# Attention stage: both transposed halves of a unit in one burst, and four more planner steps at the start

## The chip, the core and the metric

The kernel runs on one core of a Trainium2 chip. The core has a matrix engine (TensorE, PE in the profile, with its weight loads as PEld), a vector engine (DVE), a scalar engine (ACT), GpSimd (POOL), and a sync engine (SP) that issues most transfers. Each engine takes its instructions in order; they wait for each other by semaphores. Matrix products go into PSUM, from which ACT and DVE read them.

The metric is the time of one execution in device microseconds; the median of several runs counts. A profile is of one further execution, whose own time stands beside its span below.

## What is computed

One transformer-like block on a sequence of 1024 tokens, width 1024: a modulated RMS norm, one wide projection, attention beside a bidirectional state-space scan, a gated merge, and an MLP. The part that matters here is the attention: 16 query heads over 4 key heads, head width 64, all in float32, and the sigmoid gates that are merged later.

```python
q, k, v, xBC, z, dt_raw, gates = jnp.split(proj, offsets, axis=-1)
...
def one_block(qi):
    sc = jnp.einsum("bqgrd,bkgd->bgrqk", qi, k).astype(jnp.float32) * scale
    p = jax.nn.softmax(sc, axis=-1).astype(v.dtype)
    return jnp.einsum("bgrqk,bkgd->bqgrd", p, v)
...
g_attn = jax.nn.sigmoid(gates[..., :D_MODEL])
g_ssd = jax.nn.sigmoid(gates[..., D_MODEL:])
merged = g_attn * (attn @ w_attn_out[l]) + g_ssd * (ssd @ w_ssd_out[l])
```

## The kernel before

The kernel goes through stages: projections, convolution, attention, scan with the attention's output product, merge, and the MLP. To keep float32 accuracy with faster products, a matrix is often split into a high part (rounded by ACT, `A.copy` at L173) and the rest (a subtraction on DVE, `tt` at L159); the helper `split` does both, so these two lines stand for many places, and the tiles' names tell them apart.

The change is in the attention stage. Two generators, each a stream of PE work, are interleaved there:

- `attn_stream` goes through 128 **units**: 16 heads by 8 blocks of 128 queries. Four units make a **band** of 512 queries.
- `gates_stream` computes columns of the gate projection, 11 blocks of 16 steps, three matmuls a step (tile `psg`, L211 to L213; in the text G). Its weights are loaded by SP (L186), split by ACT and POOL; its results are copied by ACT (`ost`, L1006) and stored from ACT's queue.

`weave` (the planner) sees only the costs that the streams yield. Each stream has a total; at each point the one whose share of its total is smaller goes on until its next yield. The stage is a manual schedule for PE: PE's instructions stand in its queue in exactly the order in which the streams issue them. The instructions of the other engines are ordered when the program is built, by when their inputs and buffers are ready, those written earlier first.

For a unit u the stream does:

- `scores(u)`, S in the text: four matmuls of 512 columns into a PSUM tile `pss` (L1042, L1044; two such tiles); DVE takes the negative row maximum `nm` (L1046); ACT writes the exponentials into `pf` (L1048; two such tiles) and their sums. S runs two units ahead.
- `turn(u, hf)`, T0 and T1: for each half of the 1024 keys four 128 x 128 transposes of `pf` into a PSUM tile `pst` (L1059). There are two `pst`; one comes free when `split` has made `ph` (ACT) and `pl` (DVE) of it. A buffer of a tag goes to whichever tile asks next once one is free. `ph` and `pl` hold one half of a band (four units side by side), with three buffers each, so a band takes two.
- `values(b, hf)`, V: the second products, 16 matmuls a band, given out four at a time by `all_values`. They come one band after the transposes, in the four units of the next band, and are summed in the one tile `pv` (L1096 to L1099). The first four matmuls and the next four (units 4k and 4k+1 of the next band) read the first half's `ph` and `pl`, the others the second half's. After the last, ACT copies `ax` and DVE adds `av`. The first four units have no V, since no band is complete.
- once a head, at every eighth unit, `sums`: one transpose of the reciprocal sums into a `pst` tile (L1070; Z in the text), copied by ACT as `zr`; then loads and POOL's division.

In the order before, V and any G that the planner gives out stand between T0 and T1. Totals: 128 x 2.72 + 18 for the attention (a unit yields 0.92 for S, 0.44 for each half, 0.92 for V), 114.4 for the gates (176 steps at 0.65).

Of the kernel before, what the change touches and what calls it, by code (L numbers as in the profile page):

```python
# [34 lines left out]
GATES_EARLY = 11  # L35
LEAD2 = 0
# [4 lines left out]
L0 = 18  # L41
# [22 lines left out]
def weave(tc, *streams, lead=0):  # L64


    st = [[g, float(total), 0.0, i] for i, (g, total) in enumerate(streams)]
    while st:
        for s in sorted(st, key=lambda e: e[2] / e[1]):
            try:  # L70
                if s[3] == 0 and lead:
                    with tc.high_priority(offset=lead):
                        cost = next(s[0])
                else:
                    cost = next(s[0])
            except StopIteration:
                st.remove(s)
                break
            if cost is not None:
                s[2] += cost  # L80
                break
        else:
            raise RuntimeError("no stream can go on")
# [8 lines left out]
def block(ctx: ExitStack, tc: tile.TileContext, ia, out, upto=99, dbg=None):  # L92
    nc = tc.nc
    V, A, G, T = nc.vector, nc.scalar, nc.gpsimd, nc.tensor
# [77 lines left out]
    def split(hi, lo, src, e_hi=None, e_lo=None):  # L172
        (e_hi or A.copy)(hi, src)  # L173
        tt(e_lo or V, lo, src, hi.bitcast(F32), ALU.subtract)
# [17 lines left out]
    def w_cols(w, c0, k0=0):  # L192
        return w[k0 * P:(k0 + KT) * P, c0:c0 + P].rearrange("(k p) c -> p k c", p=P)

    def gemm_cm(ps_pool, tag, wsrcs, ahi, alo, evac, bufs=None, pair=False, then=None, e_lo=None):

        ws = {0: load_w(wsrcs[0], e_lo=e_lo)}
        if then:
            then()
        n = len(wsrcs)  # L200
        order = [(i, h) for i in range(n) for h in range(2)]
        if pair:
            order[:4] = [(0, 0), (1, 0), (0, 1), (1, 1)]
        for i, half in order:
            if half == 0 and i + 1 < n and i + 1 not in ws:
                ws[i + 1] = load_w(wsrcs[i + 1], e_lo=e_lo)
            hi, lo = ws[i]
            if 1:
                ps = ps_pool.tile([P, 512], F32, name=tag, tag=tag, bufs=bufs)
                for k in range(KT):  # L210
                    T.matmul(ps, hi[:, k], ahi[k][half], start=k == 0, stop=False)  # L211
                    T.matmul(ps, hi[:, k], alo[k][half], start=False, stop=False)  # L212
                    T.matmul(ps, lo[:, k], ahi[k][half], start=False, stop=k == KT - 1)  # L213
                    yield 0.65
                evac(i, half, ps)
# [783 lines left out]
    with tc.tile_pool(name="p3k", bufs=1, reuse_waits="tile") as p3k, \  # L999
# [3 lines left out]
        def gates_stream(pool, psp, i0, i1, bufs=2, e_lo=None):  # L1003
            def evac(i, half, ps):
                st = pool.tile([P, 512], F32, name="ost", tag="ost", bufs=2)
                A.copy(st, ps)  # L1006
                adma(gt_d[i0 + i][:, half * 512:(half + 1) * 512], st)

            yield from gemm_cm(psp, "psg", [w_cols(w_in, OFF_G + i * P) for i in range(i0, i1)], hhi, hlo, evac, bufs=bufs, e_lo=e_lo)

        def attn_stream():
# [5 lines left out]
            def load_head(h):  # L1017
                g = h // 4
                if h % 4 == 0:
                    k1, k2, v1 = (p3k.tile(shp, F32R, name=nm, tag=nm, bufs=2)  # L1020
                                  for nm, shp in (("k1", [P, S]), ("k2", [P, S]), ("v1", [P, NT, P])))
                    dma(k1.bitcast(F32), k1_d[g])
                    kv[g] = k1, k2, v1
                qs[h] = p3k.tile([P, S], F32R, name="q1", tag="q1", bufs=2)
                dma(qs[h].bitcast(F32), q1_d[h])
                if h % 4 == 0:
                    dma(k2.bitcast(F32), k2_d[g])
                    dma(v1.bitcast(F32), v1_d[g])
# [6 lines left out]
            def scores(u):  # L1035
                h, t = divmod(u, NT)
                q1 = qs[h]
                k1, k2, _ = kv[h // 4]
                ps = ps3.tile([P, S], F32, name="pss", tag="pss", bufs=2)
                ts = slice(t * P, (t + 1) * P)  # L1040
                for n in range(2):
                    T.matmul(ps[:, n * 512:(n + 1) * 512], q1[:, ts], k1[:, n * 512:(n + 1) * 512], start=True, stop=False)  # L1042
                for n in range(2):
                    T.matmul(ps[:, n * 512:(n + 1) * 512], q1[:, ts], k2[:, n * 512:(n + 1) * 512], start=False, stop=True)  # L1044
                nm = nms.pop() if nms else p3.tile([P, 1], F32, name="nm", tag="nm", bufs=4)
                V.tensor_reduce(out=nm, in_=ps, axis=AX.X, op=ALU.max, negate=True)  # L1046
                pfs[u] = p3.tile([P, S], F32, name="pf", tag="pf", bufs=2)
                A.activation(pfs[u], ps, AF.Exp, bias=nm, accum_out=zall[:, u:u + 1])  # L1048

            def turn(u, hf):  # L1050

                pf = pfs[u]
                b, j = divmod(u, 4)
                if j == 0:
                    phs[b, hf] = p3.tile([P, 4, 512], F32R, name="ph", tag="ph", bufs=3)
                    pls[b, hf] = p3.tile([P, 4, 512], F32R, name="pl", tag="pl", bufs=3)
                pt = ps3.tile([P, 4, P], F32, name="pst", tag="pst", bufs=2)
                for k in range(4):
                    T.transpose(pt[:, k], pf[:, (hf * 4 + k) * P:(hf * 4 + k + 1) * P], ident)  # L1059
                js = slice(j * P, (j + 1) * P)  # L1060
                split(phs[b, hf][:, :, js], pls[b, hf][:, :, js], pt)
# [3 lines left out]
            def sums(h):  # L1065

                zi = p3.tile([P, NT], F32, name="zi", tag="zi", bufs=1)
                V.reciprocal(zi, zall[:, NT * h:NT * h + NT])
                pz = ps3.tile([P, 4, P], F32, name="pst", tag="pst", bufs=2)
                T.transpose(pz[0:NT, 0], zi, ident)  # L1070
                zr = p3.tile([NT, P], F32, name="zr", tag="zr", bufs=1)
                A.copy(zr, pz[0:NT, 0])
                adma(rz_d[h].rearrange("(t p) -> t p", p=P), zr)

            def sums_back(h):

                rzs[h] = p3.tile([HD, S], F32, name="rz", tag="rz", bufs=1)
                dma(rzs[h], rz_d[h].partition_broadcast(HD))

            def divide(b):  # L1080
                h, av, hs = b // 2, avs.pop(b), slice((b % 2) * 512, (b % 2 + 1) * 512)
                tt(G, av, av, rzs[h][:, hs], ALU.mult)

                (adma if h == NH - 1 else dma)(av_d[h // 2][(h % 2) * HD:(h % 2 + 1) * HD, hs], av)
# [25 lines left out]
            def all_values(b):  # L1110
                for hf in range(2):
                    yield from values(b, hf)

            NU = NH * NT
# [7 lines left out]
            pvq = iter(())  # L1122
            for u in range(NU + 4):
                if u % NT == 4 and 1 < u // NT + 1 < NH:
                    load_head(u // NT + 1)
                if u + 2 < NU:
                    scores(u + 2)
                    yield 0.92
                for hf in range(2):
                    if u < NU:  # L1130
                        turn(u, hf)
                        yield 0.44
                    if hf == 0:
                        c = next(pvq, None)
                        if c:
                            yield c
                h = u // NT - 1
                if h >= 0:
                    if u % NT == 0:
                        sums(h)  # L1140
                    elif u % NT == 1:
                        sums_back(h)
                    elif u % NT in (2, 3):
                        divide(2 * h + u % NT - 2)
                if u % 4 == 3 and u < NU:
                    pvq = all_values(u // 4)

        with tc.manual_schedule(engines=M2):
            weave(tc, (attn_stream(), 128 * 2.72 + L0), (gates_stream(p3, ps3, 0, GATES_EARLY, 1, G), GATES_EARLY * 10.4), lead=LEAD2)
    if upto <= 3:  # L1150
        return dict(gt_d=gt_d, av_d=av_d, rz_d=rz_d)

# [896 lines left out]
```

## Time and profile before

| what | us |
|---|---|
| median of 3 runs | 2447.72 (2446.38 to 2450.83) |
| the profiled execution, its own time | 2451.32 |
| span of the profile | 2449.5 |
| PE busy in the span | 2377.3 |
| DVE busy | 1702.4 |
| ACT busy | 1091.8 |
| POOL busy | 827.9 |
| the attention stage, from the first transpose to the last | 685.3 to 1176.2 |

The span is that of the instructions in the trace; the 1.8 us to the execution's own time lie around it. Busy times of PE overlap from one matmul to the next, so that a full PE shows as 97% or more and small waits inside it do not show at once. In a timeline row stand the start, the length, the engine, the line, the operation, what is written from what, the shape and the count; in brackets the idle time of the engine before it and what ended it.

### The profile page before, as it was taken

To read this page: it belongs to the slowest core of one execution; us is meant where nothing else is said; L and a number is where in the kernel's file an instruction comes from. 1 tells how busy PE (TensorE), PEld (TensorE's weight loads), DVE (VectorE), ACT (ScalarE), POOL (GpSimd) and SP (SyncE) were. 2 spreads that over 40 slices of the span, in tenths; PEclk is the share of its full clock that TensorE was granted. 3 is DMA by queue.
4 is the path that set the end of the run, shared out by engine and by line. 5 is a ranking of instruction groups with operands and counts; after the bars stand their busy time and mean duration, and the time that the engine had idled before them with its cause. 6 is when DMAs were issued, how large, how long until landed. Compare 5 with 4: busy or idle time off the path is not lost.

```text
span 2449.5 us, 32244 instructions
## 1 busy us (share of the span) xinstructions
PE 2377.3 (97%) x11307; PEld 1899.4 (78%) x11307; DVE 1702.4 (69%) x2325; ACT 1091.8 (45%) x1884; POOL 827.9 (34%) x637
## 2 busy tenths in 40 slices
PE   8999999999989999999989999999999999999999
PEld 4998877888867777777767767787787888788887
DVE  5876435777756666666577796557568888768794
ACT  5455413555566666666333343344242222364430
POOL 0221107666611111110356666534006786123200
PEclk9999999999999999999999999999999999999999
DMA  7664841333531212111667765476325554654422
GB/s 255 181 184 147 259 167 65 95 104 112 185 112 52 91 52 81 57 54 48 219 205 228 221 208 176 146 270 205 132 74 194 185 197 163 234 171 138 157 79 82
DMA packets 288595, 366.53 MB, mean 150 GB/s; under 512 B 33961, under 2 KB 168849, under 8 KB 288433
## 3 DMA queue, kind: packets, MB, share of 16 engines
q1 hardware_dynamic: 216246, 288.77, 37.2%
q10 hardware_dynamic: 72187, 75.70, 9.3%
q8 instruction: 90, 1.47, 0.2%
q14 instruction: 72, 0.59, 0.1%
HBM read 250.54 MB, written 113.84 MB: 149 GB/s over the span
## 4 chain that ended last, share of the span: by engine, by line
PE 80%; DVE 8%; DMA 5%; issue 2%; ACT 2%; POOL 2%; SPq 0%; ACTq 0%; DVEq 0%; POOLq 0%
PE pst L1059 5%; PE psg L211 4%; PE psg L213 4%; PE psg L212 4%; PE p L1928 3%; PE p L1927 3%; PE p L1926 3%; PE psc L919 3%; PE psc L920 3%; PE psc L921 3%; PE psq L519 3%; PE psq L520 3%; PE psq L518 3%; PE pp L1514 3%; PE pp L1512 3%; PE pp L1513 3%
## 5 line engine op out<-in xcount | busy, mean ns | idle before, releaser
L1046 DVE TENSOR_REDUCE nm<-pss 128x1 f32<-128x1024 f32 x128 | 156.7, 1225 | 125.1 <-PE pss L1044 123.5
L1048 ACT ACTIVATE pf<-pss,nm 128x1024 f32<-128x1024 f32 x128 | 143.0, 1117 | 98.8 <-PE pst L1059 96.1
L159 DVE TENSOR_TENSOR pl<-pst,ph 128x512 fp32r<-128x512 f32 x256 | 167.6, 683 | 27.1 <-ACT ph L173 27.1
L1059 PEld LDWEIGHTS pst<-masks,pf 128*128 128x128 f32 x1024 | 117.8, 140 | 73.8 <-issue 33.9
L519 PE MATMUL psq<-twl,hh 128*128 128x512 f32 (+1 forms) x448 | 168.3, 377 | 2.5 <-DVE twl L159 2.5
L1059 PE MATMUL pst<-masks,pf 128*128 128x128 f32 x1024 | 157.4, 276 | 13.3 <-DVE pl L159 10.8
L173 ACT CAST ph<-pst 128x512 fp32r<-128x512 f32 x256 | 145.9, 586 | 54.5 <-PE pst L1059 37.9
L518 PE MATMUL psq<-twh,hh 128*128 128x512 f32 (+1 forms) x448 | 166.8, 376 | 3.5 <-ACT twh L173 3.5
L520 PE MATMUL psq<-twh,hl 128*128 128x512 f32 (+1 forms) x448 | 167.4, 375 | 0.0
L159 POOL TENSOR_TENSOR av<-av,rz 64x512 f32<-64x512 f32 x32 | 42.0, 1315 | 346.4 <-DMA rz<-rz 141.2
L1926 PE MATMUL p<-o,o 128*128 128x512 f32 x400 | 153.6, 390 | 3.3 <-ACT o L173 1.9
L1927 PE MATMUL p<-o,o 128*128 128x512 f32 x400 | 155.3, 389 | 0.2 <-DVE o L159 0.2
L1928 PE MATMUL p<-o,o 128*128 128x512 f32 x400 | 153.7, 389 | 0.0
L173 ACT CAST wop<-ws 128x512 fp32r<-128x512 f32 x116 | 71.2, 621 | 127.5 <-PE pp L1514 52.4
L865 DVE SCALAR_TENSOR_TENSOR tap<-pad,cwT,tap 128x1024 f32<-128x1024 f32 x96 | 123.4, 1285 | 4.9 <-ACT tap L863 3.5
L159 POOL TENSOR_TENSOR ws<-r,r 128x512 f32<-128x512 f32 x29 | 41.7, 1438 | 215.2 <-DVE ro L159 151.0
L159 POOL TENSOR_TENSOR sl<-sl 128x512 f32<-128x512 f32 x32 | 49.6, 1553 | 179.1 <-DVE o L159 72.7
L173 ACT CAST o<-sl 128x512 fp32r<-128x512 f32 x92 | 56.9, 622 | 104.7 <-PE p L1928 88.7
L1097 PE MATMUL pv<-pl,v 128*64 128x512 f32 x256 | 101.5, 417 | 0.0
L159 DVE TENSOR_TENSOR o<-sl,o 128x512 fp32r<-128x512 f32 x92 | 72.3, 788 | 39.8 <-ACT o L173 39.8
L211 PE MATMUL psg<-hh,whi 128*128 128x512 f32 x224 | 95.3, 425 | 1.2 <-ACT ost L1006 1.2
L518 PEld LDWEIGHTS psq<-twh,hh 128*128 128x128 f32 x448 | 84.8, 189 | 14.6 <-ACT twh L173 3.9
(457 smaller groups left out, 7026.4 us busy)
## 6 DMA issues: line engine op xcount, KB each, us to landing
ar<-r SPq DMA_DIRECT2D x100, 256.0 KB
wada<-in_w_ada_dram SPq DMA_DIRECT2D x48, 512.0 KB
r<-in_w_mlp_dram SPq DMA_DIRECT2D x32, 512.0 KB
sl<-in_w_mlp_dram SPq DMA_DIRECT2D x64, 256.0 KB
r<-in_w_in_dram SPq DMA_DIRECT2D x26, 512.0 KB
r<-ro ACTq DMA_DIRECT2D x49, 256.0 KB
r<-as SPq DMA_DIRECT2D x48, 256.0 KB
xb<-cst ACTq DMA_DIRECT2D x20, 512.0 KB
```

What stands on the lines that cost most here:

```text
L159: e.tensor_tensor(out=o, in0=a, in1=b, op=op)
L173: (e_hi or A.copy)(hi, src)
L211: T.matmul(ps, hi[:, k], ahi[k][half], start=k == 0, stop=False)
L518: T.matmul(o, hhi[k][half][:, sl], hi[:, k % 2, :n], start=k == 0, stop=False)
L519: T.matmul(o, hhi[k][half][:, sl], lo[:, k % 2, :n], start=False, stop=False)
L520: T.matmul(o, hlo[k][half][:, sl], hi[:, k % 2, :n], start=False, stop=k == KT - 1)
L1046: V.tensor_reduce(out=nm, in_=ps, axis=AX.X, op=ALU.max, negate=True)
L1048: A.activation(pfs[u], ps, AF.Exp, bias=nm, accum_out=zall[:, u:u + 1])
L1059: T.transpose(pt[:, k], pf[:, (hf * 4 + k) * P:(hf * 4 + k + 1) * P], ident)
L1926: T.matmul(ps, a[:, 0, sl], b[0], start=start, stop=False)
L1927: T.matmul(ps, a[:, 0, sl], b[1], start=False, stop=False)
L1928: T.matmul(ps, a[:, 1, sl], b[0], start=False, stop=stop)
```

## The change

Both halves of a unit are transposed one behind the other, with one yield of 0.88 for the two; V comes after them. In units 0 to 3, where there is no V, the stream yields 0.92 all the same without issuing anything, so that the planner gives out gate products there. The attention's total grows by these four yields.

```diff
                 if u + 2 < NU:
                     scores(u + 2)
                     yield 0.92
-                for hf in range(2):
-                    if u < NU:
-                        turn(u, hf)
-                        yield 0.44
-                    if hf == 0:
-                        c = next(pvq, None)
-                        if c:
-                            yield c
+                if u < NU:
+                    turn(u, 0)
+                    turn(u, 1)
+                    yield 0.88
+                c = next(pvq, 0.92 if u < 4 else None)
+                if c:
+                    yield c
...
-            weave(tc, (attn_stream(), 128 * 2.72 + L0), (gates_stream(p3, ps3, 0, GATES_EARLY, 1, G), GATES_EARLY * 10.4), lead=LEAD2)
+            weave(tc, (attn_stream(), 128 * 2.72 + 4 * 0.92 + L0), (gates_stream(p3, ps3, 0, GATES_EARLY, 1, G), GATES_EARLY * 10.4), lead=LEAD2)
```

## The prediction

> **What bounds the kernel now.** I read the shares of the chain that ended last, then the table by stretches of time over the attention stage, then the timeline of single units and the list of waits. In the table the columns are the stretch, its length, the busy time of PE, its weight loads, DVE, ACT and POOL, the granted clock, and the DMA share with its GB/s.
>
> ```profile
> PE 80%; DVE 8%; DMA 5%; issue 2%; ACT 2%; POOL 2%; SPq 0%; ACTq 0%; DVEq 0%; POOLq 0%
> ```
>
> ```profile
> 685.00:698.00 13.00, 8.99 (x53) 7.02 (x53) 8.86 (x11) 7.98 (x15) 0.00 (x0) 1.00 0.16 48
> 698.00:1177.00 479.00, 468.86 (x2482) 355.21 (x2481) 327.14 (x419) 319.05 (x571) 60.92 (x39) 1.00 0.20 60
> 1182.00:1245.00 63.00, 53.01 (x211) 39.02 (x209) 42.48 (x56) 18.11 (x32) 26.28 (x24) 0.92 0.86 280
> ```
>
> In the steady part (698 to 1177 us) PE is the only full engine; DVE and ACT are busy for about two thirds of it, DMA for a fifth. So a change of the order counts only by PE's waits. "Busy" hides some of them, because a matmul lasts longer than the step to the next. I therefore count by steps. The chain of waits gives 0.23 us for a matmul of 512 columns (two in 0.47) and 0.109 us for a transpose (16 in 1.75):
>
> ```profile
> 857.12 0.47 PE pss L1042 x2
> ```
>
> ```profile
> 1771.84 1.75 PE pst L1543 x16
> ```
>
> A **band** is four units, whose second products (V, four matmuls a unit) come one band later. Per unit the order is scores S (four matmuls), transposes T0 and T1 (four each, the halves), V, and gate products G (three matmuls) wherever the planner's fractions put them. By the yields that is 2.72/366.16 x 114.4/0.65 = 1.31 G a unit, 5.23 a band. The timeline of one unit 4k+1, the second of a band (start, length, engine, line):
>
> ```profile
> 858.08 1.23 DVE L1046 TENSOR_REDUCE nm<-pss 128x1 f32<-128x1024 f32 x1 [1.14 <-PE pss L1044]
> ...
> 858.57 0.60 PE L1059 MATMUL pst<-masks,pf 128*128 128x128 f32 x4
> ...
> 858.92 0.48 PE L1097 MATMUL pv<-pl,v 128*64 128x512 f32 x1
> ...
> 859.21 0.59 ACT L173 CAST ph<-pst 128x512 fp32r<-128x512 f32 x1 [0.79 <-PE pst L1059]
> 859.24 0.40 PE L1099 MATMUL pv<-ph,v 128*128 128x512 f32 x1
> ...
> 859.71 0.39 PE L1099 MATMUL pv<-ph,v 128*128 128x512 f32 x1
> 859.82 0.69 DVE L159 TENSOR_TENSOR pl<-pst,ph 128x512 fp32r<-128x512 f32 x1 [0.52 <-ACT ph L173]
> 860.19 0.59 ACT L173 CAST ph<-pst 128x512 fp32r<-128x512 f32 x1 [0.40 <-PE pv L1099]
> 860.57 0.66 PE L1059 MATMUL pst<-masks,pf 128*128 128x128 f32 x4 [0.47 <-DVE pl L159]
> 860.81 0.69 DVE L159 TENSOR_TENSOR pl<-pst,ph 128x512 fp32r<-128x512 f32 x1 [0.29 <-ACT ph L173]
> ```
>
> Four transposes cost 0.44 here: from 858.57 to the second matmul behind them at 859.24 is 0.67, less one matmul step. The same place (T0 of a unit 4k+1) in the second band and thirty bands later:
>
> ```profile
> 703.29 0.60 PE L1059 MATMUL pst<-masks,pf 128*128 128x128 f32 x4
> ...
> 703.49 1.22 DVE L1046 TENSOR_REDUCE nm<-pss 128x1 f32<-128x1024 f32 x1 [1.69 <-PE pss L1044]
> ...
> 704.63 0.68 DVE L159 TENSOR_TENSOR pl<-pst,ph 128x512 fp32r<-128x512 f32 x1
> ...
> 705.36 0.66 PE L1059 MATMUL pst<-masks,pf 128*128 128x128 f32 x4
> ```
>
> ```profile
> 1167.92 0.60 PE L1059 MATMUL pst<-masks,pf 128*128 128x128 f32 x4
> ```
>
> A band takes (1167.92 - 703.29)/30 = 15.49 us. Its work is 32 matmuls of S and V plus 15.7 of G at 0.23 (10.97), and eight bursts at 0.44 (3.52): 14.5. So PE waits **0.98 us a band**, 30 us over 31 bands. This is all that any order of this stage can win.
>
> **The change part by part.** First, the burst by itself. Eight transposes at 0.109 and two bursts of four at 0.44 are both 0.88 us; joining them saves nothing. No instruction is added or removed, and no DMA: the gate weights' loads and the gates' stores shift with their products by under a unit.
>
> Second, what no longer lies between the halves.:
>
> ```profile
> ACT ph L173 <- PE pv L1099: 15.9, 31, 1.1
> PEld pst L1059 <- DVE pl L159: 15.6, 34, 1.0
> PE pst L1059 <- DVE pl L159: 10.8, 18, 1.6
> ```
>
> PE and its weight loads wait for DVE's pl, and ACT's copy ph waits for a V matmul 31 times, once a band. The reason is in the code: ph and pl have three buffers, a band takes two, and the second of the new band gets the one that V of units 4k and 4k+1 still reads. So ph of unit 4k's second half can be written only after V(4k+1). Until then its PSUM tile, one of the two named pst, stays taken (860.19: ph starts after V's last matmul). T1(4k+1) therefore gets the pst buffer of T0(4k+1): it starts at 860.57, right after that half's pl (859.82 to 860.51), and before the older one (860.81). From T0's last start (858.90, three steps of 0.11 after 858.57) the way is: fill 0.27 (the 0.60 of the row less 0.33), ph 0.59, pl 0.69, and three hand-overs: 1.67 us. At 703.29 no G stood between S and T0, the row maximum was on DVE when ph was done, and the way is 1.74 (703.62 to 705.36).
>
> Before, V(4k+1) and often a G ran in that time. After, T1 stands directly behind T0, and V(4k+1) behind T1 on PE's queue. T1 cannot have the other buffer at all, since that waits for V(4k+1). So **PE stands for 1.67 to 1.74 less one step of 0.11** in each of 31 bands. Writing out the order that the yields give, 17 of them have S directly before T0 (1.63) and 14 a G between (1.56): mean 1.60.
>
> Behind the waiting T1 on PE stand V(4k+1), a G, and S(4k+4); ph(4k,1) waits for that V, pl for ph, and the next burst T(4k+2) for pl. How ACT orders such work, one half earlier, is seen here: the exponential first, then both ph, then both pl, then a burst:
>
> ```profile
> 853.60 1.12 ACT L1048 ACTIVATE pf<-pss,nm 128x1024 f32<-128x1024 f32 x1 [0.55 <-PE pst L1059]
> ...
> 854.70 1.06 ACT L173 CAST ph<-pst 128x512 fp32r<-128x512 f32 x2
> ...
> 855.67 1.28 DVE L159 TENSOR_TENSOR pl<-pst,ph 128x512 fp32r<-128x512 f32 x2
> ...
> 856.49 0.63 PE L1059 MATMUL pst<-masks,pf 128*128 128x128 f32 x4
> ```
>
> From T1's last start (0): exponential 0.32 to 1.42; V directly behind T1 ends at 1.19; ph(4k,1) 1.42 to 2.00; pl 2.04 to 2.72. PE meanwhile does V, G, S and reaches T(4k+2) at 2.64: it waits 0.14, and its second half 0.17 for the second pl. With the G before the V, V ends at 1.88 and pl at 3.22; PE arrives at 2.64 (wait 0.64 + 0.17), or with a second G at 3.33 (0.12). Counted in the order: 18 x 0.31, 3 x 0.81, 9 x 0.12, so 0.29 a band.
>
> The other two bursts of a band lose a wait. Now T1's pst has to come back through exponential, ph and pl by the next T1, which costs about 0.1 in many units (856.49 is such a one: the G matmul before it started at 856.15). After, ph of the first half can go before the exponential, and 2.6 us of V, G and S lie between bursts. I take 0.40 a band for all that is left there: the eighth unit's Z transpose, which now meets a pst buffer still in use (0.3 to 1), V's buffer pv waiting for av, and the gate copies. Bounds: nothing, and the 0.98 that a whole band waits today.
>
> Third, the first four units, which have no V. Before, their halves stand together or with one G between:
>
> ```profile
> 691.35 0.60 PE L1059 MATMUL pst<-masks,pf 128*128 128x128 f32 x4
> ...
> 693.52 0.63 PE L1059 MATMUL pst<-masks,pf 128*128 128x128 f32 x4 [1.57 <-DVE pl L159]
> ```
>
> This row also shows on the chip what two halves in one burst do when no pst is free: 1.57 us idle. The new costs bring five G into these units in place of three. Followed through with the same durations, the scores of unit 4 come 0.3 us later with 2 x 0.69 = 1.4 us more done: a gain of 1 us, with bounds 0 and 1.4. At the tail, the last two bursts have no S before them and pl(124,1) comes late: a loss of about 2 (bounds 0 and 3).
>
> **Sum.** A band: 14.5 + 1.60 + 0.29 + 0.40 = 16.8 against 15.49, +1.31; times 31 is +41; -1 at the start, +2 at the tail: **+42 us**. The stage behind begins with loads that are issued as the attention's buffers come free, and nothing in it absorbs a later start. The profiled execution took 2451.32 (span 2449.5), so 2493 by it; the median of the runs is 3.6 lower, so **2490 us**.
>
> **Rivals.** (a) Faster. If T1(4k+1) found a free pst, through ph(4k,1) no longer waiting for V or PE passing V before T1, the burst would cost nothing, most waits of 0.1 would go, and with 0.29 to 0.40 left of 0.98 a band the stage would win 20 us: 2427. Against it: the 31 waits, and the place in the order. It decides where T1 starts less than 1.1 us after T0's last start; the rows say 1.67. Chance 0.04.
>
> (b) No change: the 31 new waits (50 us) are balanced by the 30 us of today's and 20 more that I fail to see: 2448. Against it, PE has no more idle time in the stage. Chance 0.02.
>
> (c) Slower by less: all other waits vanish, 31 x (1.56 - 0.98) = +18: 2466. Chance 0.12. (d) Slower by more: T(4k+2) always pays 0.81 and the rest 0.98: 31 x (1.63 + 0.81 + 0.98 - 0.98) = +76, 2523. Chance 0.12.
>
> (e) The clock falls. In 1182 to 1245, with waits and a DMA share of 0.86, it was 0.92; at that rate the 450 us of PE work (31 x 14.5) would take 39 more: 2529. Against it, 685 to 698 holds two waits of about 1.6 and was granted 1.00. Chance 0.02. The Trainium skill, "TensorE: Matmul & The Clock Gate", HAM oscillation, puts the fall of the clock at PE gaps over about 3.4 us; the 1.00 row agrees, and by that rule (e) would have no chance. The same page, A second HAM failure mode: psum-queue depth-cycling, says that short but frequent idling between matmul groups can make the clock swing too, which speaks against this change; no row before shows it.
>
> **How the numbers follow.** My forecast has 0.68. The range goes from (c) to (d), 2466 to 2523. A measurement of this kernel tells 0.2%, 5 us, from no change; chances: faster 0.04, within 0.02, slower 0.94.
>
> **What would show it.** In the changed profile T1 of each unit 4k+1 starts 1.67 to 1.75 after T0's last start with nothing between, released by DVE's pl, and a band takes about 16.8 us. ACT's ph still waits for PE's pv 31 times, now longer. Wrong would be a PE order in which V stands between the halves, a T1 released at once, or a band under 15.5.

## The result and the profile after

The changed kernel takes 2527.44 us (median of 4 runs, 2526.75 to 2528.62) against 2447.32 of the kernel before (median of 4, 2446.38 to 2450.83): a ratio of 1.0325, with an interval of 1.0313 to 1.0338, or 80 us more. The forecast was 2490 with a range up to 2523. The sign and the first wait came out as forecast. The forecast size, 42 us, was about half of the measured one, because a second wait was put far too small.

The page of the changed kernel, its busy times (share of the span, instructions):

```profile
PE 2381.2 (94%) x11307; PEld 1907.1 (76%) x11307; DVE 1708.5 (68%) x2325; ACT 1092.2 (43%) x1884; POOL 828.4 (33%) x637
```

The work is the same (PE 2381.2 against 2377.3 us), but PE's share of the span falls from 97% (2377.3 of 2449.5) to 94%. The profiled execution took 2526.75, its span is 2524.8: 75.3 us longer than before.

The table by stretches of the changed kernel (stretch, length, busy time of PE, weight loads, DVE, ACT and POOL, granted clock, DMA share, GB/s):

```profile
685.00:698.00 13.00, 13.00 (x78) 11.04 (x77) 10.85 (x14) 10.92 (x22) 0.92 (x1) 1.00 0.13 35
...
698.00:1255.00 557.00, 472.99 (x2468) 363.39 (x2467) 324.83 (x417) 317.24 (x567) 59.09 (x39) 1.00 0.17 52
```

The start (685 to 698) is now full: 13.00 of 13.00 where PE was busy for 8.99. The steady part, which now reaches to about 1255, has PE busy for 473 of 557 us at a granted clock of 1.00. So the lost time is PE standing still, and it isn't the clock. The list of waits of the changed kernel over the stage (who waits for whom: us, times, the longest):

```profile
ACT ph L173 <- PE pst L1059: 138.6, 117, 2.6
...
PE pst L1059 <- DVE pl L159: 78.1, 63, 2.2
...
PEld pst L1059 <- DVE pl L159: 72.3, 61, 2.5
...
ACT ph L173 <- PE pv L1099: 4.3, 11, 0.4
```

PE's transposes wait for DVE's pl 63 times for 78.1 us; before it was 18 times for 10.8. That is about twice a band, where the forecast had one long wait a band. The timeline shows both (first the start of the stage, then unit 37, a 4k+1, and unit 38, a 4k+2; the rows at 699.35 and 1239.47 are T0 of units 5 and 125):

```profile
690.28 1.03 PE L1059 MATMUL pst<-masks,pf 128*128 128x128 f32 x8
...
699.35 0.60 PE L1059 MATMUL pst<-masks,pf 128*128 128x128 f32 x4
...
844.25 0.60 PE L1059 MATMUL pst<-masks,pf 128*128 128x128 f32 x4
...
844.89 0.59 ACT L173 CAST ph<-pst 128x512 fp32r<-128x512 f32 x1 [2.62 <-PE pst L1059]
845.60 0.68 DVE L159 TENSOR_TENSOR pl<-pst,ph 128x512 fp32r<-128x512 f32 x1
...
846.33 0.66 PE L1059 MATMUL pst<-masks,pf 128*128 128x128 f32 x4 [1.48 <-DVE pl L159]
...
848.21 0.40 PE L1099 MATMUL pv<-ph,v 128*128 128x512 f32 x1
...
848.65 1.07 ACT L173 CAST ph<-pst 128x512 fp32r<-128x512 f32 x2 [0.36 <-PE pv L1099]
...
849.27 0.69 DVE L159 TENSOR_TENSOR pl<-pst,ph 128x512 fp32r<-128x512 f32 x1 [0.75 <-ACT ph L173]
...
849.88 1.22 DVE L1046 TENSOR_REDUCE nm<-pss 128x1 f32<-128x1024 f32 x1
...
850.05 0.62 PE L1059 MATMUL pst<-masks,pf 128*128 128x128 f32 x4
...
851.01 1.28 DVE L159 TENSOR_TENSOR pl<-pst,ph 128x512 fp32r<-128x512 f32 x2
...
851.84 0.63 PE L1059 MATMUL pst<-masks,pf 128*128 128x128 f32 x4 [1.16 <-DVE pl L159]
...
1239.47 0.60 PE L1059 MATMUL pst<-masks,pf 128*128 128x128 f32 x4
```

The burst at 690.28 is one of the first units: eight transposes in a row, 1.03 us, nothing in the way. T0 of unit 37 starts at 844.25, its last transpose at 844.58 (three steps of 0.11 later), and T1 at 846.33: 1.75 later, after ph (844.89) and pl (845.60 to 846.28). This is the wait that was forecast. Then a G and V(37) run, V's last matmul ends at 848.61, and ph of the held half goes at 848.65. Two ph follow one behind the other (units 36 and 37), but their two pl do not: the row maximum of the next scores (849.88) takes 1.22 us of DVE between them. The second pl starts at 851.01, and T1 of unit 38, whose place on PE is at 850.49 (850.05 and four steps of 0.11), starts at 851.84: 1.35 us of waiting where the forecast had 0.12 for such a band (a G ahead of V and another behind it).

Not every band looks like this one. What counts is where DVE has the row maximum at that point. In 11 of the 31 bands, those with a G ahead of V but two, it stands between the two pl, as above. In five it stands ahead of both, here behind unit 21 (both halves of unit 22 are one row):

```profile
775.57 1.23 DVE L1046 TENSOR_REDUCE nm<-pss 128x1 f32<-128x1024 f32 x1 [0.37 <-PE pss L1044]
...
776.71 1.28 DVE L159 TENSOR_TENSOR pl<-pst,ph 128x512 fp32r<-128x512 f32 x2
...
777.45 1.31 PE L1059 MATMUL pst<-masks,pf 128*128 128x128 f32 x8 [1.22 <-DVE pl L159]
```

In 14 it comes behind both, so that the two pl run as the forecast had them in every band, here behind unit 53:

```profile
920.55 1.29 DVE L159 TENSOR_TENSOR pl<-pst,ph 128x512 fp32r<-128x512 f32 x2 [0.27 <-ACT ph L173]
...
921.30 1.32 PE L1059 MATMUL pst<-masks,pf 128*128 128x128 f32 x8
...
921.76 1.22 DVE L1046 TENSOR_REDUCE nm<-pss 128x1 f32<-128x1024 f32 x1
```

There T(4k+2) waits 0.4 us, in the 11 and the five bands about 1.55 each. The last band has no maximum and waits 1.8, since its V comes late.

A band takes (1239.47 - 699.35)/30 = 18.00 us, against 15.49 before and 16.8 forecast.

**Where the whole loss is.** I counted PE's waits over the stage as the prediction did: each start-to-start step less that of an unhindered one (0.23 behind a matmul of 512 columns, 0.109 between transposes; at a change of kind 0.313 for the second step behind a transpose, 0.028 for the first). In us, each row from one profiled execution, for the two kernels and the experiments below ("4k, 4k+3" is T1 of these units; T(4k+2) is both its halves; the rest is the other bursts, G, S, Z and the end):

| kernel | units 0-3 | T1(4k+1) | T(4k+2) | T1 of 4k, 4k+3 | V | rest | total |
|---|---|---|---|---|---|---|---|
| before | 4.7 | 8.0 | 5.7 | 8.8 | 0.7 | 7.2 | 35.1 |
| after | 0.1 | 52.4 | 32.6 | 13.5 | 4.6 | 7.4 | 110.6 |
| e1_burst_only | 0.1 | 51.7 | 33.6 | 12.4 | 3.2 | 6.4 | 107.4 |
| e2_start_only | 3.4 | 9.1 | 5.7 | 8.4 | 0.8 | 6.5 | 33.9 |
| e3_second_split | 0.1 | 9.4 | 47.4 | 13.6 | 4.7 | 5.8 | 81.0 |
| e4_second_merged | 3.4 | 52.4 | 16.1 | 8.3 | 2.0 | 8.8 | 91.0 |
| e5_after_dve | 0.1 | 52.3 | 14.7 | 0.6 | 11.8 | 6.3 | 85.8 |
| e6_after_four | 0.1 | 1.5 | 7.9 | 13.6 | 4.5 | 5.7 | 33.3 |
| e7_after_one | 0.1 | 53.0 | 32.4 | 13.6 | 6.0 | 7.0 | 112.1 |
| e8_before_act | 0.4 | 8.1 | 0.7 | 2.1 | 1.8 | 7.8 | 20.9 |
| e9_after_four_act | 0.1 | 0.5 | 0.1 | 0.0 | 8.4 | 5.8 | 14.9 |
| e10_before_four_act | 0.4 | 0.0 | 0.2 | 2.1 | 1.8 | 7.3 | 11.8 |

110.6 less 35.1 is 75.5, and the spans differ by 75.3. So these waits are the whole loss, and none of it came from another stage.

### The profile page after: what moved, and what is told of

Same layout as the page of the kernel before. It is cut to its first block, busy times and chain, and to the rows that moved or that the text cites. A ratio compares the mean times of both kernels' runs of the same rounds, so it can differ in the third digit from the quotient of the medians.

```text
span 2524.8 us, 32168 instructions
## 1 busy us (share of the span) xinstructions
PE 2381.2 (94%) x11307; PEld 1907.1 (76%) x11307; DVE 1708.5 (68%) x2325; ACT 1092.2 (43%) x1884; POOL 828.4 (33%) x637
## 5 line engine op out<-in xcount | busy, mean ns | idle before, releaser
L1059 PE MATMUL pst<-masks,pf 128*128 128x128 f32 x1024 | 148.9, 277 | 79.4 <-DVE pl L159 78.1
L159 POOL TENSOR_TENSOR sl<-sl 128x512 f32<-128x512 f32 x32 | 49.6, 1553 | 178.5 <-DVE o L159 72.1
L518 PEld LDWEIGHTS psq<-twh,hh 128*128 128x128 f32 x448 | 84.6, 189 | 13.6 <-ACT twh L173 2.9
```

Of the source, the lines that this page charges most:

```text
L159: e.tensor_tensor(out=o, in0=a, in1=b, op=op)
L518: T.matmul(o, hhi[k][half][:, sl], hi[:, k % 2, :n], start=k == 0, stop=False)
```

## The experiments

**Theory.** The burst does the damage. It takes away the work between T0 and T1 that covered the way of a pst buffer back through ph and pl; in unit 4k+1 the other buffer is held besides, because ph and pl have three buffers. **Rival one**: the planner's new steps move the gate products into bad places. **Rival two**: any burst of eight costs, in whatever unit it stands.

**e1: the burst alone; e2: the start steps alone.** Two kernels that take the change apart.

```diff
# e1, against the kernel after
-                c = next(pvq, 0.92 if u < 4 else None)
+                c = next(pvq, None)
...
-(attn_stream(), 128 * 2.72 + 4 * 0.92 + L0)
+(attn_stream(), 128 * 2.72 + L0)
# e2, against the kernel before
-                        c = next(pvq, None)
+                        c = next(pvq, 0.92 if u < 4 else None)
...
-(attn_stream(), 128 * 2.72 + L0)
+(attn_stream(), 128 * 2.72 + 4 * 0.92 + L0)
```

> The burst in every unit, without the four added planner steps at the start. All theories: nearly the whole loss, 2526 to 2532 us against 2527 of the changed kernel. If the added steps caused part of the loss, it would be under 2520.

> The four added planner steps alone, the halves of a unit stay apart as before. My theory: the first four units wait less, 2443 to 2447 us against 2447 of before. If more gate products at the start cost something later, over 2450.

Measured: e1 2522.58 against 2449.45 of before, 1.0298 (1.0283 to 1.0313); e2 2449.91, 1.0001 (0.9991 to 1.001). The burst is the loss, which rules out rival one. Both missed their expected time by a little. The start steps by themselves are worth nothing that can be measured: the first four units' waits only fall from 4.7 to 3.4. In e1, without these steps, they fall to 0.1, so the gain at the start belongs to the burst. With the burst, the steps seem to cost some 3 us (107.4 to 110.6 in the table, spans of 2522.0 and 2524.8); this is close to what can be told, and I did not follow it further.

**e3: all units in bursts except 4k+1; e4: only 4k+1 in a burst.** The unit with the held buffer is taken out of the change, or is the only one in it.

```diff
# e3, against the kernel after; e4 has u % 4 != 1 in both places
                     turn(u, 0)
-                    turn(u, 1)
-                    yield 0.88
+                    if u % 4 == 1:
+                        yield 0.44
+                    else:
+                        turn(u, 1)
+                        yield 0.88
                 c = next(pvq, 0.92 if u < 4 else None)
                 if c:
                     yield c
+                if u < NU and u % 4 == 1:
+                    turn(u, 1)
+                    yield 0.44
```

> As the changed kernel, but in the second unit of each band (4k+1) the halves stay apart with V between them. My theory (the burst of unit 4k+1 waits for its own first half, because ph and pl have three buffers, and the next burst pays for the late V): the 52 us of waits in T1(4k+1) fall to about 8 and the 33 us of T(4k+2) to about 6, so 2450 to 2462 us. Rival (eight transposes in one go cost everywhere, wherever they stand): three quarters of the 80 us stay, over 2500 us.

> As the kernel before with the four added steps, but the halves of unit 4k+1 alone in one burst. My theory: nearly the whole loss comes from these 32 units, 2505 to 2520 us. Rival (the cost is of every burst): a quarter of the 80 us, 2465 to 2470 us.

Measured: e4 2506.99, 1.0232 (1.0215 to 1.0249), a hit: one unit in four, joined, brings the larger part of the loss (T1(4k+1) 52.4, as in after). e3 2498.44, 1.0198 (1.0183 to 1.0213), a miss by far: T1(4k+1) fell to 9.4 as the theory wanted, but T(4k+2) rose to 47.4. The two losses add to more than the change as a whole, so they are not two independent prices. The timeline of e3, T1 of unit 37 and then unit 38:

```profile
838.54 0.66 PE L1059 MATMUL pst<-masks,pf 128*128 128x128 f32 x4
...
838.69 0.69 DVE L159 TENSOR_TENSOR pl<-pst,ph 128x512 fp32r<-128x512 f32 x1 [0.21 <-ACT ph L173]
...
839.28 1.12 ACT L1048 ACTIVATE pf<-pss,nm 128x1024 f32<-128x1024 f32 x1 [0.62 <-PE pst L1059]
...
840.16 1.22 DVE L1046 TENSOR_REDUCE nm<-pss 128x1 f32<-128x1024 f32 x1 [0.78 <-PE pss L1044]
...
840.39 0.58 ACT L173 CAST ph<-pst 128x512 fp32r<-128x512 f32 x1
...
840.65 0.60 PE L1059 MATMUL pst<-masks,pf 128*128 128x128 f32 x4
...
841.41 1.24 DVE L159 TENSOR_TENSOR pl<-pst,ph 128x512 fp32r<-128x512 f32 x2
...
842.20 0.63 PE L1059 MATMUL pst<-masks,pf 128*128 128x128 f32 x4 [0.95 <-DVE pl L159]
```

Here V stands before T1(37), so only S and one G (838.95 to 840.65) lie between T1(37) and the burst of unit 38. The buffer that T1(37) filled comes back after exponential (839.28), ph (840.39), maximum (840.16) and pl (841.41 to 842.0), over 3 us after T1 began; T1(38) has its place at 841.09 and starts at 842.20. So the theory as I had it does not fit. The total comes within 2 us of rival two's 2500, but the place does not fit that rival: over half of the waits stand in one unit of four. The better reading: **every pst needs 1.7 to 3.5 us to come back, by whatever stands on ACT's and DVE's queues; a burst takes both buffers, and the work behind it must cover the way of both.** Splitting one unit moves the cover from behind it to inside it and uncovers the next unit.

**e5: the maximum behind the pl.** The order on DVE's queue can be changed by itself. The maximum of S(u) is put behind the second half's pl of unit u-3, in three units of four.

```diff
+                if u >= 3 and (u - 3) % 4 in (1, 2, 3):
+                    with tc.issue_after(last[u - 3, 1]):
+                        V.tensor_reduce(out=nm, in_=ps, axis=AX.X, op=ALU.max, negate=True)
+                else:
                     V.tensor_reduce(out=nm, in_=ps, axis=AX.X, op=ALU.max, negate=True)
...
-                split(phs[b, hf][:, :, js], pls[b, hf][:, :, js], pt)
+                A.copy(phs[b, hf][:, :, js], pt)
+                ins = V.tensor_tensor(out=pls[b, hf][:, :, js], in0=pt, in1=phs[b, hf][:, :, js].bitcast(F32), op=ALU.subtract)
+                last[u, hf] = getattr(ins, "ins", ins)
```

> The changed kernel, with one order on DVE set by hand: the row maximum of the scores two units ahead stands behind the second half's pl of the unit before (units 4k+1, 4k+2, 4k+3), not ahead of it. Theory D (the 33 us of waits at T(4k+2) come from the maximum standing ahead of pl on DVE's queue): they fall to 9 to 15, and 2495 to 2510 us. Rival K (they come from the late V(4k+1) alone): 2520 to 2530 us.

Measured: 2501.92 against 2449.31, 1.0217 (1.0203 to 1.0231), a hit, and 25.5 us under the change as it is (27.1 by the spans of the two profiles). The same units 37 and 38 in e5's timeline (T1 of unit 37, then the rows that were apart in the changed kernel):

```profile
840.46 0.66 PE L1063 MATMUL pst<-masks,pf 128*128 128x128 f32 x4 [1.48 <-DVE pl L1066]
...
842.77 1.07 ACT L1065 CAST ph<-pst 128x512 fp32r<-128x512 f32 x2 [0.36 <-PE pv L1105]
...
843.39 1.29 DVE L1066 TENSOR_TENSOR pl<-pst,ph 128x512 fp32r<-128x512 f32 x2 [0.75 <-ACT ph L1065]
...
844.17 1.28 PE L1063 MATMUL pst<-masks,pf 128*128 128x128 f32 x8
...
844.59 1.22 DVE L1048 TENSOR_REDUCE nm<-pss 128x1 f32<-128x1024 f32 x1
```

The two pl now stand together (x2, 1.29 us), the maximum comes after them, and the eight transposes of unit 38 are one row: 1.28 us where an unhindered burst takes 1.03. T1(37) waits its 1.48 as before. T(4k+2) falls from 32.6 to 14.7 and T1 of 4k and 4k+3 from 13.5 to 0.6, and part is given back: V's waits for its buffer pv, which DVE's `av` empties, rise from 4.6 to 11.8. In all, this one change of order on DVE is worth 24.8 us of PE's waits (110.6 to 85.8). In e5 the maximum comes behind both pl in 30 bands, and T(4k+2) waits 0.4 in 26 of them, as in the 14 bands of the changed kernel that had this order already.

**e6: a fourth buffer for ph and pl; e7: its control.** With four, ph of the second half need not wait for V(4k+1). The memory for it comes from leaving out two loads, in both kernels.

```diff
# e6 and e7
-                    k1, k2, v1 = (p3k.tile(shp, F32R, name=nm, tag=nm, bufs=2)
-                                  for nm, shp in (("k1", [P, S]), ("k2", [P, S]), ("v1", [P, NT, P])))
+                    k1 = p3k.tile([P, S], F32R, name="k1", tag="k1", bufs=2)
+                    k2, v1 = k1, k1.rearrange("p (t c) -> p t c", c=P)
...
-                    dma(k2.bitcast(F32), k2_d[g])
-                    dma(v1.bitcast(F32), v1_d[g])
# e6 alone
-                    phs[b, hf] = p3.tile([P, 4, 512], F32R, name="ph", tag="ph", bufs=3)
-                    pls[b, hf] = p3.tile([P, 4, 512], F32R, name="pl", tag="pl", bufs=3)
+                    phs[b, hf] = p3.tile([P, 4, 512], F32R, name="ph", tag="ph", bufs=4)
+                    pls[b, hf] = p3.tile([P, 4, 512], F32R, name="pl", tag="pl", bufs=4)
```

> The changed kernel with four buffers of ph and pl instead of three. To make room it leaves out the loads of k2 and v1 and reads k1 in their place, with the same matmuls in number and shape. My theory (three buffers make T1(4k+1) wait for its own first half): the waits at T1(4k+1) fall from 52 us to under 10 and those at T(4k+2) with them, 2445 to 2465 us. Rival (two pst are too few for eight transposes, whatever ph and pl do): over 2490 us.

> The control to the run with four buffers: the changed kernel with three buffers that also leaves out the loads of k2 and v1 and reads k1 in their place. Both theories: as the changed kernel, 2515 to 2530 us, so that the loads are worth nothing.

Measured: e6 2448.81, 0.9998 (0.9989 to 1.0007); e7 2529.73 in a single run. Both as expected: the left-out loads are worth nothing, the fourth buffer about 80 us. The timeline of e6, unit 37 and the burst of unit 38:

```profile
823.57 1.04 PE L1056 MATMUL pst<-masks,pf 128*128 128x128 f32 x8
...
824.21 1.08 ACT L173 CAST ph<-pst 128x512 fp32r<-128x512 f32 x2 [2.52 <-PE pst L1056]
...
824.91 1.28 DVE L159 TENSOR_TENSOR pl<-pst,ph 128x512 fp32r<-128x512 f32 x2
...
825.17 1.13 ACT L1045 ACTIVATE pf<-pss,nm 128x1024 f32<-128x1024 f32 x1
...
827.67 1.03 PE L1056 MATMUL pst<-masks,pf 128*128 128x128 f32 x8
```

Both bursts run through (1.04 and 1.03), both ph follow at once, ahead of the exponential, and both buffers are back before the next burst. T1(4k+1) falls to 1.5 us and T(4k+2) to 7.9. So both large waits need the missing ph buffer: it holds a pst until V, and the late pl in the next unit is its echo. By e5, over half of that echo needs the maximum's place on DVE as well.

**e8: the exponential behind the ph.** In the kernel before, ACT's exponential of unit u+2 stands ahead of the ph of T1(u), and so holds its pst for another 1.1 us. In e8 it is issued behind both halves of unit u; all else is as before.

```diff
-                A.activation(pfs[u], ps, AF.Exp, bias=nm, accum_out=zall[:, u:u + 1])
+                wait_exp[u] = ps, nm
+                if u < 2:
+                    expo(u)
...
+            def expo(u):
+                ps, nm = wait_exp.pop(u)
+                A.activation(pfs[u], ps, AF.Exp, bias=nm, accum_out=zall[:, u:u + 1])
...
                         turn(u, hf)
                         yield 0.44
+                        if hf and u + 2 < NU:
+                            expo(u + 2)
```

> The kernel before, with the exponential of two units ahead written behind both halves of the unit, so that ACT makes the second half's ph before it. If the waits of about 0.1 us at T1 come from the exponential standing ahead of ph on ACT: 14 us of waits in T1 of units 4k, 4k+2 and 4k+3 fall to about 2, 2433 to 2440 us. If they are hand-overs that no order changes, or the later exponential makes the scores wait: 2445 us or more.

Measured: 2439.82, 0.9959 (0.9946 to 0.9973), a hit. This kernel does the whole computation and is faster than both. Its timeline, T1 of a unit, the ph of it, and only then the exponential:

```profile
850.69 0.66 PE L1066 MATMUL pst<-masks,pf 128*128 128x128 f32 x4 [0.48 <-DVE pl L159]
...
851.38 0.59 ACT L173 CAST ph<-pst 128x512 fp32r<-128x512 f32 x1 [0.50 <-PE pst L1066]
...
851.86 1.12 ACT L1055 ACTIVATE pf<-pss,nm 128x1024 f32<-128x1024 f32 x1
...
852.00 0.69 DVE L159 TENSOR_TENSOR pl<-pst,ph 128x512 fp32r<-128x512 f32 x1 [0.39 <-ACT ph L173]
```

The buffer filled at 850.69 is back at 852.7, two microseconds later. The waits of T(4k+2) and of T1 in 4k and 4k+3 fall from 14.5 to 2.8; T1(4k+1), which hangs on the three buffers, stays at 8.1.

**e9 and e10: with every pst quickly back, is a burst worth anything?** Both have the fourth buffer of e6 and the exponential of e8; e9 has them on the kernel after, e10 on the kernel before.

> The changed kernel with four buffers of ph and pl and with the exponential written behind both halves, so that ACT makes both ph ahead of it. Leaves out the loads of k2 and v1 and reads k1 in their place. My theory (the burst itself costs and saves nothing; only the return of pst counts): the 21 us of waits left at T1 of units 4k, 4k+2 and 4k+3 fall under 5, 2428 to 2436 us. If those waits had another cause: 2445 us or more.

> The same two edits on the kernel before, where V stands between the halves (loads of k2 and v1 left out, k1 read in their place). My theory (the burst itself is worth nothing): within 5 us of the kernel with the burst and the same edits, 2428 to 2438 us. Rival (one burst a unit saves PE time, one change between transposes and matmuls less): the kernel with the burst is faster by 10 us or more.

Measured: e9 2429.5, 0.9927 (0.9913 to 0.994); e10 2427.95, 0.9914 (0.99 to 0.9927), against 2449.79. As expected, they are alike. The timelines give T0 of units 5 and 125, of e9

```profile
698.66 1.03 PE L1063 MATMUL pst<-masks,pf 128*128 128x128 f32 x8
...
1146.65 1.04 PE L1063 MATMUL pst<-masks,pf 128*128 128x128 f32 x8
```

and of e10:

```profile
699.25 0.60 PE L1063 MATMUL pst<-masks,pf 128*128 128x128 f32 x4
...
1145.26 0.60 PE L1063 MATMUL pst<-masks,pf 128*128 128x128 f32 x4
```

A band takes (1146.65 - 698.66)/30 = 14.93 us in e9 and (1145.26 - 699.25)/30 = 14.87 in e10, near the 14.5 of work that the prediction counted. When nothing waits for pst any more, eight transposes in one burst are worth nothing against two fours. That rules out rival two as well: the bursts of e9 run in 1.03 us. What is left in e9 is mostly V's wait for `av` (8.4).

The full computation with four buffers was not run; these kernels have the room for it only from the loads that they leave out. It stays open whether the 12 us between e8 and e10 can be had in another way.

## Why the prediction was right in sign and short in size

- **The bound.** PE is full in the steady part, and only its waits count: right. The waits in the stage differ by 75.5 us and the spans by 75.3. Today's waits were put at 30 us for 31 bands; by the table they are 35.1 less 4.7 at the start and 0.6 at the end, 29.8.
- **The burst by itself costs and saves nothing** (0.88 both ways): right, as e9 and e10 show.
- **T1(4k+1) waits for its own first half, 1.60 a band**: right in place, cause and size. 31 x 1.60 = 49.6 forecast, 52.4 measured. The cause, three buffers of ph and pl, is shown by e6, where it falls to 1.5.
- **T(4k+2), 0.29 a band: this is the step that failed.** The prediction let "ph(4k,1) 1.42 to 2.00; pl 2.04 to 2.72" run into the next burst and gave the second half 0.17 "for the second pl": two pl in a row on DVE, with no maximum in the way. On DVE's queue the next row maximum, 1.22 us, stands between them in 11 bands and ahead of both in five. So T(4k+2) paid 32.6 us, 1.05 a band, where 9 were forecast: 24 of the 33 us that the forecast was short. The 11 bands paid 17 us and the five 8. The 14 bands in the order that was forecast paid 5.6, 0.4 each, close to the forecast. e5 puts the maximum behind both pl, and T(4k+2) falls to 14.7: by that run the maximum is 18 of the 24 us. The other 6 were not taken apart further. The row from which I took the order (two pl in one row of 1.28 us at 855.67) did show two pl together, but a maximum had run just ahead of them, which the prediction left out:

```profile
854.52 1.22 DVE L1046 TENSOR_REDUCE nm<-pss 128x1 f32<-128x1024 f32 x1 [0.71 <-PE pss L1044]
```

- **The rest of a band, 0.40**: too low. It is 24.4 us (110.6 less 0.1, 52.4, 32.6 and 1.1 at the end), 0.79 a band, against 12.4. I expected T1 of 4k and 4k+3 to lose their waits, because "ph of the first half can go before the exponential"; they went from 8.8 to 13.5 instead. In e5 they are 0.6, so the same maximum on DVE is behind it. V's wait for `av` rose as well (0.7 to 4.6).
- **Start and end**: -1 forecast and -4.6 measured (4.7 to 0.1), by the burst and not by the new steps (e1, e2), outside the bounds given and for a reason that stays open; +2 forecast at the end and 0.5 measured (0.6 to 1.1).
- The terms that were off add up: 2.8 + 23.6 + 12 - 3.6 - 1.5 is 33.3, and 42 + 33.3 is the 75.3 of the spans (to the tenth by chance, since the 42 is rounded).
- **The rivals.** (d), "T(4k+2) always pays 0.81 and the rest 0.98", was the nearest. Its place was right, its price at T(4k+2) too low and its rest too high (1.05 and 0.79 measured); the range ended 4 us short. Of (a), a free pst would have cost nothing, e6 shows the condition but not the gain: 2448.81 is no faster than before, since other waits stay, 13.6 us of them at T1 of 4k and 4k+3. Only e9, with the exponential moved too, has the gain: 2429.5. (e), the clock: the table by stretches shows 1.00 through 557 us with a wait of about 1.6 us in every band. The Trainium skill, "TensorE: Matmul & The Clock Gate", A second HAM failure mode: psum-queue depth-cycling, speaks of frequent short idling between matmul groups that makes the clock swing; this trace does not show it for one such wait in each 18 us and a shorter second one.
- **The signs.** T1(4k+1) at 1.67 to 1.75 behind T0 came out as forecast (a mean of 1.74 over 31 bands, with one of 2.49). A band of about 16.8 us did not: it is 18.00. The 31 waits of ACT for pv did not either: there are 11, 4.3 us in all. The forecast contradicted itself here: by its own clock V ends at 1.19 and the exponential at 1.42 where no G stands before V, so ACT cannot be seen waiting in those 18 bands. All 11 are bands with a G there.

The Trainium skill, "Perfetto Trace Analysis", Identifying Performance Opportunities, Optimization Strategy, reads a gap that repeats on the engine that should be full as a possible lack of SBUF or PSUM for the next tile. The runs agree, with 81 us for one more buffer (e7 to e6). They add that the order of other engines' queues makes such a gap with the same buffers: e5 and e8 change no buffer and win 25.5 and 9.5 us.

## What to carry to other kernels

Before joining two pieces of work on a full engine, write down for each of its output buffers the whole way back: who reads it, what stands ahead of that reader on its queue, and what that reader itself waits for. The work left between two uses must cover that way, and the burst needs as many free buffers as it fills. If a wait cannot be covered by order on the full engine, look at the order on the others: a long instruction that nobody is waiting for (here the exponential, 1.1 us, and the maximum, 1.2) standing ahead of a short one that frees a buffer can cost the full engine up to its length. Here the maximum cost about 1.15 us in each of 16 bands, the exponential about 0.1 at each of three bursts a band. Moving it changes no work at all, though part of the gain can come back as another wait (V's for pv in e5).

## What the runs showed of the hardware that was not expected

That joining bursts saves nothing was forecast from the steps; e9 and e10 show it in time. There PE goes from matmuls to these transposes or back 255 and 503 times, and the medians differ by 1.6 us, the joined one being the slower, within their intervals. The granted clock stayed at 1.00 with PE busy by its rows for only 85% of the steady part (473 of 557 us).
